# Split weights at a place in their tiles that moves by 16 bytes from piece to piece, and three raw weight buffers for four

## The chip, the cores and the metric

The kernel runs on one core of a Trainium2 chip. The metric is the device time of one execution in microseconds (us); lower is better. Beside the timed runs there is one execution under the hardware profiler, whose trace is what the rows below come from.

## The reference

The reference is the trunk of a decoder with two mixing layers, each followed by an MLP, on one sequence of 1024 positions with 1024 features, all in float32. Every layer adds its result to x.

```
for layer in range(2):
    if layer == 0: x = x + even_mixer(rms_norm(x), ...)   # sparse attention with an indexer, and forgetting attention
    else:          x = x + odd_mixer(rms_norm(x), ...)    # latent attention, and a Mamba-2 scan
    x = x + square(relu(rms_norm(x) @ w1)) @ w2           # w1 1024x4096, w2 4096x1024
```

Each mixer is a wide input projection `h @ w_in`, the attention or scan on its columns, and an output projection `o @ w_out`. Most of the arithmetic is in these matrix products with weights.

## The kernel before

Positions are worked on in two halves of 512, features in chunks of 128 on the partitions. A product with weights has to be as exact as float32 at the price of a single-pass format, so both operands are split into a rounded high part and a low part that holds the rest, and `mm3` (L271) adds three matmuls: high by high, high by low, low by high. L273, L274 and L275 are these three lines, and most of TensorE's work.

Weights come in pieces. `piece` (L282) cuts a weight block into sub-pieces of at most 1024 columns per partition (four chunks of 256 columns as a rule), 512 KB each. For each sub-piece it takes a tile `wraw` (four buffers), `whi` and `wlo` (three buffers each), loads `wraw` by a DMA on SyncE's queue (L295), and calls `split` (L254): ScalarE (ACT) writes `whi` as the rounded copy of `wraw` (L257), then VectorE (DVE), or GpSimd (POOL) in the first layer's start, writes `wlo = wraw - whi` (L258). 414 sub-pieces are handled in the whole run, one after the other through the same buffers. A `wraw` buffer is free again when its `wlo` is written, a `whi` or `wlo` buffer when the last matmul on it is done. All tiles of these tags have 4096 bytes per partition, as have those of the normed x (`xnh`, `xnl`), of the hidden values (`h`) and of the general pool.

Two functions consume pieces. `proj_f` (L302) keeps a weight slice of 128 columns stationary and streams 512 positions of x past it; it serves the MLP (`mlp`, L477, and `add_rows`, L454), the output projections and part of the input projections. `proj_t` (L315) keeps a block of 128 positions stationary and streams 256, 384 or 512 weight columns. In the trace `pm<-xnh,whi` means that the result `pm` has `xnh` moving and `whi` stationary. One piece is narrow: L691 joins 72 and 4 columns to rows of 76, so its slices for the eight chunks start 304 bytes apart in the tile.

The order of the work on each engine follows the program text, in which generators for attention and scan are advanced beside the projections by `tick`; the framework's scheduler sets semaphores and buffer waits, and may move an instruction up where an earlier one is not ready. SyncE's queue carries all weight loads, the rows of x (L77), constants (L112, L136) and the output (L1401), in order. POOL's queue carries values parked in DRAM.

Of the kernel before, what the change touches and what calls it, by code (L numbers as in the profile page):

```python
# [11 lines left out]
F32 = mybir.dt.float32  # L12
F32R = mybir.dt.float32r
# [6 lines left out]
P = 128  # L20
# [16 lines left out]
def trunk(ctx, tc, a, out):  # L37
# [7 lines left out]
    wp = ctx.enter_context(tc.tile_pool(name="wp", bufs=4))  # L45
# [208 lines left out]
    def split(hi, lo, src, scale=None, eng=None):  # L254

        if scale is None:
            act.activation(hi, src, AF.Copy)  # L257
            (eng or dve).tensor_sub(lo, src, hi.bitcast(F32))  # L258
        else:
            act.activation(hi, src, AF.Copy, scale=scale)  # L260
            dve.scalar_tensor_tensor(lo, src, scale, hi.bitcast(F32), op0=ALU.mult, op1=ALU.subtract)
# [15 lines left out]
    def rstd_of(ssq, n, over, name):  # L277

        pool.tensor_scalar(ssq, ssq, 1.0 / over, EPS, op0=ALU.mult, op1=ALU.add)
        pool.tensor_tensor(ssq, ssq, mhalf[:, :n], op=ALU.pow)  # L280

    def piece(parts, kc, n):  # L282


        subs = []
        per = min(kc, 1024 // n)
        for k0 in range(0, kc, per):
            nk = min(per, kc - k0)
            raw, hi, lo = (wp.tile([P, 1024], dt, name=nm, tag=nm, bufs=bufs)[:, :nk * n]
                           .rearrange("p (k f) -> p k f", k=nk)  # L290
                           for nm, dt, bufs in (("wraw", F32, 4), ("whi", F32R, 3), ("wlo", F32R, 3)))
            at = 0
            for ap in parts:
                w = ap.shape[-1]
                nc.sync.dma_start(raw[:, :, at:at + w], ap[k0 * P:(k0 + nk) * P].rearrange("(k p) f -> p k f", p=P))  # L295
                at += w
            split(hi, lo, raw, eng=lo_of[0])
            lo_of.append(lo_of.pop(0))
            subs.append((k0, nk, hi, lo))
        return subs  # L300
# [153 lines left out]
    def add_rows(half, w, hs, last=None, late=0):  # L454

        for n in range(4):
            subs = piece([w[:, n * 256:(n + 1) * 256]], len(hs), 256)
            if late and n == 0:
                (k0, nk, hi, lo), = subs
                cut = nk - late  # L460
                subs = [(k0, cut, hi[:, :cut], lo[:, :cut]), (k0 + cut, late, hi[:, cut:], lo[:, cut:])]

            def done(ps, c):
                x = xc(half, c)
                dve.tensor_add(x, ps, x)  # L465
                if last is not None:
                    last(c)

            proj_f((lambda k: hs[k][0], lambda k: hs[k][1]), subs,
                   [(m * P, P, lambda ps, c=n * 2 + m: done(ps, c)) for m in range(2)])  # L470
            yield
# [5 lines left out]
    def mlp(half, layer, xn, last=None):  # L477
        w1, w2 = a["mlp_w1"][layer], a["mlp_w2"][layer]
        n_blocks = DFF // 512
        hs = {}  # L480

        def up(n):
            w = piece([w1[:, n * 256:(n + 1) * 256]], 8, 256)
            pair = [new_h(), new_h()]

            def done(ps, h):
                r = tmp(name="relu")
                act.activation(r, ps, AF.Relu)  # L488
                sq = tmp(name="rsq")
                pool.tensor_mul(sq, r, r)  # L490
                split(h[0], h[1], sq)

            proj_f(xn, w, [(m * P, P, lambda ps, h=pair[m]: done(ps, h)) for m in range(2)])
            hs[n] = pair

        up(0)
        yield
        for fb in range(n_blocks):
            up(2 * fb + 1)
            yield  # L500
            if fb + 1 < n_blocks:
                up(2 * fb + 2)
                yield
            yield from add_rows(half, w2[fb * 512:(fb + 1) * 512, :], hs.pop(2 * fb) + hs.pop(2 * fb + 1),
                                *((last, 2) if fb == n_blocks - 1 else ()))
# [173 lines left out]
    def qk_pair(xn, w_ap, gain, dst):  # L679

        w = piece([w_ap], 8, 256)
        st = g([P, NB, 256], name="st")
        ss = small(NB * 2, "ss")
        proj_t(xn, w, 256, lambda b, ps: head_norms(ps, b, st[:, b], ss, 2, P))
        rstd_of(ss, NB * 2, 128.0, "qk")
        for h in range(2):
            normed_T(st, 2, h, ss, dst[h], gain)
# [903 lines left out]
```

## Time and profile before

| | us |
|---|---|
| median of 2 timed runs | 2818.52 (2817.93 to 2819.11) |
| profiled execution, whole | 2821.86 |
| its span, first to last instruction | 2820.1 |
| TensorE busy in the span | 2734.5 |
| mean granted clock of TensorE | 0.989 of full speed |

The time of an execution is the span and a little around it. Busy time of an engine is the union of its instructions; lengths of matmuls overlap, as the next one starts before the end of the one before has been modelled, so the interval from start to start tells how fast they follow each other.

### The profile page before, as it was taken

The page shows a single profiled execution, that of the slowest core. Times are in us where ns is not written, and L with a number is a line of the kernel's source. Part 1 is how long each engine was busy: PE and PEld are TensorE (multiplying, and loading weights), DVE is VectorE, ACT ScalarE, POOL GpSimd, SP SyncE. Part 2 cuts the span into 40 slices and gives each one's busy share as a digit, 9 for nine tenths or more (in the row PEclk, how much of TensorE's full clock was granted, in tenths as well). Part 3 has the DMA queues.
Part 4 walks back from the last instruction along what each step waited for, and adds up shares of the span by engine and source line. Part 5 has one row for each costly group of instructions (what it writes and reads, how often), then busy time and mean ns, then how long its engine had stood idle before and what let it go on. Part 6 is the DMA issues. An engine that isn't in the chain of part 4 may idle for free.

```text
span 2820.1 us, 39104 instructions
## 1 busy us (share of the span) xinstructions
PE 2734.5 (97%) x14509; PEld 2334.4 (83%) x14509; DVE 1737.6 (62%) x3169; ACT 1256.2 (45%) x2446; POOL 743.9 (26%) x878
## 2 busy tenths in 40 slices
PE   7889999999999999999999999999999999999999
PEld 6888877888788898888888889888887788788887
DVE  5775456877864577764667666775467754634444
ACT  4665334599834345543333334554333323332322
POOL 5335433111100113331344410233134430110110
PEclk8999999999999999999999999999999999999999
DMA  5243433334422425853334452685433463333332
GB/s 175 75 132 120 154 111 90 105 105 142 142 69 67 164 84 156 237 184 113 113 112 140 168 185 84 178 239 177 133 97 115 136 220 94 116 97 97 98 97 68
DMA packets 302964, 365.84 MB, mean 130 GB/s; under 512 B 40611, under 2 KB 258606, under 8 KB 302774
## 3 DMA queue, kind: packets, MB, share of 16 engines
q1 hardware_dynamic: 236550, 223.51, 25.7%
q0 software_dynamic: 66224, 139.84, 15.3%
q8 instruction: 114, 1.87, 0.3%
q14 instruction: 76, 0.62, 0.1%
HBM read 292.16 MB, written 68.70 MB: 128 GB/s over the span
## 4 chain that ended last, share of the span: by engine, by line
PE 75%; DVE 9%; issue 6%; ACT 5%; POOL 3%; DMA 0%; POOLq 0%; DVEq 0%; ACTq 0%
PE pm L273 22%; PE pm L274 22%; PE pm L275 21%; PE po L548 2%; PE pa L537 2%; ACT junk L822 1%; PE pa L514 1%; DVE xr L450 1%; DVE wlo L258 1%; PE py L1339 1%; ACT whi L257 1%; DVE st L659 1%; POOL xnl L258 1%; DVE x L465 1%; POOL rsq L490 1%
## 5 line engine op out<-in xcount | busy, mean ns | idle before, releaser
L257 ACT ACTIVATE whi<-wraw 128x1024 fp32r<-128x1024 f32 (+2 forms) x414 | 434.0, 1049 | 608.4 <-PE pm L274 507.3
L258 DVE TENSOR_TENSOR wlo<-wraw,whi 128x1024 fp32r<-128x1024 f32 (+1 forms) x369 | 462.4, 1253 | 208.0 <-ACT whi L257 189.6
L273 PE MATMUL pm<-xnh,whi 128*128 128x512 f32 (+1 forms) x1360 | 547.1, 403 | 6.1 <-ACT xnh L257 4.9
L274 PE MATMUL pm<-xnl,whi 128*128 128x512 f32 (+1 forms) x1360 | 534.0, 393 | 8.6 <-DVE xnl L258 4.8
L275 PE MATMUL pm<-xnh,wlo 128*128 128x512 f32 (+1 forms) x1360 | 533.5, 392 | 0.0
L273 PE MATMUL pm<-h,whi 128*128 128x512 f32 x1024 | 409.6, 401 | 5.1 <-DVE tk L892 4.4
L274 PE MATMUL pm<-h,whi 128*128 128x512 f32 x1024 | 402.0, 393 | 0.7 <-DVE h L258 0.7
L275 PE MATMUL pm<-h,wlo 128*128 128x512 f32 x1024 | 402.0, 393 | 0.0
L465 DVE TENSOR_TENSOR x<-pm,x 128x512 f32<-128x512 f32 x336 | 230.9, 688 | 273.0 <-PE pm L275 268.8
L490 POOL TENSOR_TENSOR rsq<-relu 128x512 f32<-128x512 f32 x128 | 165.9, 1296 | 823.7 <-ACT relu L488 754.4
L274 PEld LDWEIGHTS pm<-xnl,whi 128*128 128x128 f32 (+1 forms) x1360 | 256.3, 188 | 65.4 <-POOL xnl L258 8.2
L273 PEld LDWEIGHTS pm<-xnh,whi 128*128 128x128 f32 (+1 forms) x1360 | 256.3, 189 | 58.1 <-ACT xnh L257 6.4
L275 PEld LDWEIGHTS pm<-xnh,wlo 128*128 128x128 f32 (+1 forms) x1360 | 255.8, 188 | 55.5 <-issue 0.4
L273 PE MATMUL pm<-whi,xnh 128*128 128x256 f32 x1024 | 299.8, 293 | 0.0
L275 PE MATMUL pm<-whi,xnl 128*128 128x256 f32 x1024 | 290.5, 284 | 1.9 <-POOL xnl L258 1.0
L274 PE MATMUL pm<-wlo,xnh 128*128 128x256 f32 x1024 | 290.0, 283 | 0.0
L273 PEld LDWEIGHTS pm<-h,whi 128*128 128x128 f32 x1024 | 193.3, 189 | 43.9 <-DVE tk L892 5.1
L275 PEld LDWEIGHTS pm<-h,wlo 128*128 128x128 f32 x1024 | 193.2, 189 | 41.3 <-DVE wlo L258 0.2
L274 PEld LDWEIGHTS pm<-h,whi 128*128 128x128 f32 x1024 | 193.4, 189 | 38.8 <-DVE h L258 1.7
L258 DVE TENSOR_TENSOR h<-rsq,h 128x512 fp32r<-128x512 f32 x128 | 95.1, 743 | 181.7 <-ACT h L257 180.5
L273 PEld LDWEIGHTS pm<-whi,xnh 128*128 128x128 f32 x1024 | 196.8, 192 | 3.1 <-issue 1.0
L274 PEld LDWEIGHTS pm<-wlo,xnh 128*128 128x128 f32 x1024 | 196.7, 192 | 2.9 <-issue 1.2
(651 smaller groups left out, 4518.7 us busy)
## 6 DMA issues: line engine op xcount, KB each, us to landing
wraw<-in_mlp_w_dram SPq DMA_DIRECT2D x256, 512.0 KB
wraw<-in_ev_w_in_dram SPq DMA_DIRECT2D x44, 512.0 KB
wraw<-in_od_w_in_dram SPq DMA_DIRECT2D x40, 512.0 KB
wraw<-in_od_w_out_dram SPq DMA_DIRECT2D x24, 512.0 KB
parked<-x POOLq DMA_DIRECT2D x16, 512.0 KB, 4.0
wraw<-in_ev_w_out_dram SPq DMA_DIRECT2D x16, 512.0 KB
x<-parked POOLq DMA_DIRECT2D x16, 512.0 KB, 7.6
wraw<-in_od_w_in_dram SPq DMA_DIRECT2D x32, 256.0 KB
```

The source lines that it names most:

```text
L257: act.activation(hi, src, AF.Copy)
L258: (eng or dve).tensor_sub(lo, src, hi.bitcast(F32))
L273: pe.matmul(ps, w[0], x[0], start=first, stop=False, skip_group_check=True)
L274: pe.matmul(ps, w[0], x[1], start=False, stop=False, skip_group_check=True)
L275: pe.matmul(ps, w[1], x[0], start=False, stop=last, skip_group_check=True)
L450: dve.scalar_tensor_tensor(y, xc(half, c), gain[:, c:c + 1], box["rb"], op0=ALU.mult, op1=ALU.mult)
L465: dve.tensor_add(x, ps, x)
L490: pool.tensor_mul(sq, r, r)
L514: pe.transpose(ps[:, k * P:(k + 1) * P], p[:, (k0 + k) * P:(k0 + k + 1) * P], ident)
L537: pe.matmul(ps[:, :m], q, kf(k0, m), start=(i == 0), stop=(i == len(mats) - 1))
L548: pe.matmul(po, v(k), pt[:, k, :], start=(k == 0), stop=(k == nk - 1))
L659: dve.tensor_scalar(v, v, r[:, b * heads + h: b * heads + h + 1], None, op0=ALU.mult)
```

## The change

`piece` keeps a counter of sub-pieces modulo 32. The `whi` and `wlo` parts of a sub-piece start 4 elements (16 bytes) per count further in their tiles; after 32 sub-pieces (512 bytes) the counter starts again at 0. To have room for this, the `whi` and `wlo` tiles grow from 1024 to 1152 elements (4096 to 4608 bytes per partition). The raw tiles stay at 1024 elements and offset 0, and there are three of them in place of four. Together the three tags take 39,936 bytes per partition in place of 40,960. Nothing else is changed: the same instructions, on the same engines.

```diff
@@ -279,6 +279,8 @@
         pool.tensor_scalar(ssq, ssq, 1.0 / over, EPS, op0=ALU.mult, op1=ALU.add)
         pool.tensor_tensor(ssq, ssq, mhalf[:, :n], op=ALU.pow)
 
+    phase_of = [0]
+
     def piece(parts, kc, n):
 
 
@@ -286,9 +288,12 @@
         per = min(kc, 1024 // n)
         for k0 in range(0, kc, per):
             nk = min(per, kc - k0)
-            raw, hi, lo = (wp.tile([P, 1024], dt, name=nm, tag=nm, bufs=bufs)[:, :nk * n]
+            at = phase_of[0] * 4
+            phase_of[0] = (phase_of[0] + 1) % 32
+            raw, hi, lo = (wp.tile([P, room], dt, name=nm, tag=nm, bufs=bufs)[:, at:at + nk * n]
                            .rearrange("p (k f) -> p k f", k=nk)
-                           for nm, dt, bufs in (("wraw", F32, 4), ("whi", F32R, 3), ("wlo", F32R, 3)))
+                           for nm, dt, bufs, room, at in (("wraw", F32, 3, 1024, 0), ("whi", F32R, 3, 1152, at),
+                                                          ("wlo", F32R, 3, 1152, at)))
             at = 0
             for ap in parts:
                 w = ap.shape[-1]
```

## Rows read from the trace of the kernel before

**Rows 1.** The page: the length of the span, and under it the busy time of each engine, its share of the span in brackets and its count of instructions; then TensorE's granted clock in 40 equal slices of the span, in tenths of full speed (9 is 90% or more).
```profile
span 2820.1 us, 39104 instructions
...
PE 2734.5 (97%) x14509; PEld 2334.4 (83%) x14509; DVE 1737.6 (62%) x3169; ACT 1256.2 (45%) x2446; POOL 743.9 (26%) x878
...
PEclk8999999999999999999999999999999999999999
```

**Rows 2.** The page's chain of work that ended last, followed back from the last instruction: its shares by engine, then by line.
```profile
PE 75%; DVE 9%; issue 6%; ACT 5%; POOL 3%; DMA 0%; POOLq 0%; DVEq 0%; ACTq 0%
PE pm L273 22%; PE pm L274 22%; PE pm L275 21%; PE po L548 2%; PE pa L537 2%; ACT junk L822 1%; PE pa L514 1%; DVE xr L450 1%; DVE wlo L258 1%; PE py L1339 1%; ACT whi L257 1%; DVE st L659 1%; POOL xnl L258 1%; DVE x L465 1%; POOL rsq L490 1%
```

**Rows 3.** The groups of instructions by line with shapes kept apart, TensorE's matmuls on weights (`out<-moving,stationary`; `128*128` is the stationary block, `128x512` the result). After the bar: busy us, mean ns of one instruction from its start to its modelled end, then the idle time before them. Of each kind the L273 row alone; L274 and L275 have the same counts.
```profile
L273 PE MATMUL pm<-xnh,whi 128*128 128x512 f32 x1344 | 539.9, 403 | 3.9 <-ACT xnh L257 2.8 <-DVE sums L524 1.1
L273 PE MATMUL pm<-h,whi 128*128 128x512 f32 x1024 | 409.6, 401 | 5.1 <-DVE tk L892 4.4 <-ACT h L257 0.7
L273 PE MATMUL pm<-whi,xnh 128*128 128x256 f32 x1024 | 299.8, 293 | 0.0
...
L273 PE MATMUL pm<-y,whi 128*128 128x512 f32 x128 | 49.9, 390 | 0.4 <-DVE x L465 0.4
L273 PE MATMUL pm<-oa,whi 128*128 128x512 f32 x64 | 26.7, 419 | 0.3 <-ACT oa L257 0.3
L273 PE MATMUL pm<-oc,whi 128*128 128x512 f32 x64 | 25.1, 392 | 0.0
L273 PE MATMUL pm<-whi,low 128*128 128x384 f32 x48 | 16.5, 344 | 0.0
L273 PE MATMUL pm<-ho,whi 128*128 128x512 f32 x32 | 14.2, 444 | 0.0
L273 PE MATMUL pm<-whi,low 128*128 128x512 f32 x32 | 13.1, 410 | 2.0 <-ACT vt L1128 2.0
L273 PE MATMUL pm<-ob,whi 128*128 128x512 f32 x32 | 12.6, 393 | 0.3 <-DVE x L465 0.3
```

**Rows 4.** The timeline of TensorE in a long stretch of the last layer without a pause (start us, length us, engine, line, operation): the first and the last of fourteen matmuls in a row on 128-column weight slices.
```profile
2599.92 0.39 PE L273 MATMUL pm<-h,whi 128*128 128x512 f32 x1
...
2602.87 0.39 PE L274 MATMUL pm<-xnl,whi 128*128 128x512 f32 x1
```

**Rows 5.** The same view in a projection with the weights moving, 256 columns wide: the first and the last of nine matmuls in a row.
```profile
1819.80 0.28 PE L275 MATMUL pm<-whi,xnl 128*128 128x256 f32 x1
...
1820.76 0.28 PE L274 MATMUL pm<-wlo,xnh 128*128 128x256 f32 x1
```

**Rows 6.** The same view at the one piece whose slices are 76 columns wide (L691): from its second matmul to its last, 23 matmuls in a row.
```profile
379.93 0.40 PE L274 MATMUL pm<-xnl,whi 128*76 128x512 f32 x1
...
384.98 0.39 PE L275 MATMUL pm<-xnh,wlo 128*76 128x512 f32 x1
```

**Rows 7.** The same view right behind a pause on TensorE (four transposes came between): the third to the last matmul of one block, nine in a row.
```profile
1800.88 0.40 PE L273 MATMUL pm<-xnh,whi 128*128 128x512 f32 x1
...
1802.72 0.39 PE L275 MATMUL pm<-xnh,wlo 128*128 128x512 f32 x1
```

**Rows 8.** The same view in the stretch at the start in which the granted clock was 0.5: nine matmuls in a row.
```profile
25.50 0.63 PE L274 MATMUL pm<-xnl,whi 128*128 128x512 f32 x1
...
28.91 0.63 PE L273 MATMUL pm<-xnh,whi 128*76 128x512 f32 x1
```

**Rows 9.** The groups by line with shapes kept apart, the two halves of a split: ACT writes `whi`, DVE writes `wlo`.
```profile
L258 DVE TENSOR_TENSOR wlo<-wraw,whi 128x1024 fp32r<-128x1024 f32 x361 | 456.4, 1264 | 208.0 <-ACT whi L257 189.6 <-PE pa L1294 10.0 <-PE py L1339 4.4
L257 ACT ACTIVATE whi<-wraw 128x1024 fp32r<-128x1024 f32 x404 | 427.1, 1058 | 605.9 <-PE pm L274 505.3 <-issue 48.6 <-PE pm L275 39.2
```

**Rows 10.** Who waited for whom (us in total, times, longest us): first ACT, then, from the same view of SyncE's own queue, the issue of the weight loads.
```profile
ACT whi L257 <- PE pm L274: 507.3, 218, 11.4
SPq L295 <- DVE wlo L258: 1748.8, 295, 22.8
```

**Rows 11.** Three timelines of one steady stretch: SyncE's weight loads (five issues merged in one row, from the first start to the last end), ACT's and DVE's work on the pieces.
```profile
2560.76 22.13 SPq L295 DMA_DIRECT2D wraw<-in_mlp_w_dram  x5
2575.83 1.23 DVE L258 TENSOR_TENSOR wlo<-wraw,whi 128x1024 fp32r<-128x1024 f32 x1 [1.93 <-ACT whi L257]
2574.73 1.06 ACT L257 ACTIVATE whi<-wraw 128x1024 fp32r<-128x1024 f32 x1 [1.56 <-PE pm L274]
2580.17 1.06 ACT L257 ACTIVATE whi<-wraw 128x1024 fp32r<-128x1024 f32 x1
```

**Rows 12.** The DMA issues by tile (all from POOL's queue): count, KB of one and the median us from issue to landing, where the trace tells the landing.
```profile
parked<-x POOLq DMA_DIRECT2D x16, 512.0 KB, 4.0
...
oc<-oc POOLq DMA_DIRECT2D x8, 512.0 KB, 11.9
```

**Rows 13.** Busy time of each engine in two stretches (stretch, its us, then PE, PEld, DVE, ACT, POOL with their counts of instructions; the last three numbers are the granted clock, the busy share of the 16 DMA engines and GB/s).
```profile
1118.00:1150.00 32.00, 31.60 (x187) 28.12 (x186) 21.06 (x58) 16.39 (x51) 10.04 (x13) 1.00 0.87 224
2295.00:2320.00 25.00, 25.00 (x112) 20.69 (x111) 11.91 (x14) 4.25 (x4) 4.20 (x8) 1.00 1.09 377
```

**Rows 14.** The timelines of SyncE and TensorE around the second half's rows of x.
```profile
154.65 2.46 SPq L77 DMA_DIRECT2D xrow<-in_x_dram  x4
165.78 0.37 SPq L295 DMA_DIRECT2D wraw<-in_ev_w_in_dram  x1
171.08 1.04 PE L381 MATMUL pm<-ident,xrow 128*128 128x128 f32 x8
```

## The prediction

> **What bounds the kernel now.** I read the page's first part, then its chain, then the groups of matmuls, and only then single matmuls in the timeline. TensorE is busy for 2734.5 of 2820.1 us (97%) and the granted clock is at its upper level (2.4 GHz) in all slices but the first [rows 1]. The chain that ended last lies on TensorE for 75%, and 65% of the span is the three lines of `mm3`, L273 to L275 [rows 2]. So time can come only from the interval at which matmuls on weights follow each other, or be lost by letting TensorE wait. Who waits for weights? Not TensorE: ACT's split waits for TensorE to free a `whi` buffer (507.3 us), and SyncE's loads wait for the split to free a `wraw` buffer (1748.8 us) [rows 10]. Weights are always early.
>
> The interval is start to start; the lengths of 0.39 us overlap. In a settled stretch, 14 matmuls start within 2.95 us, 0.2269 us apiece [rows 4]; 512 columns at 2.4 GHz would be 0.2133, so 13.6 ns come on top. With 256 columns it is 0.96 us over 8 intervals, 0.1200 [rows 5], against 0.1067: 13.3 ns on top, the same for half the columns. At the lower clock, 1.2 GHz, 8 intervals take 3.41 us, 0.4263 [rows 8], against 0.4267: nothing on top. That fixed sum per matmul is what a shift of addresses could touch, as the next stationary block is read while the present moving operand is read.
>
> **The change part by part.**
>
> *Addresses of `whi` and `wlo`.* Before, every tile of the pools that hold x, hidden values and weights is 4096 bytes, and a weight slice starts at a multiple of 512 bytes in its tile (128 or 256 columns of 4 bytes, or a row of 256, 384 or 512). So both operands of nearly every `mm3` matmul have the same place modulo 512 bytes. After, the weight operand is off by 0, 16, ... 496 bytes, a new value for each of the 414 tiles, while x and the hidden values stay. The counts, three lines each [rows 3]: weights stationary under 512 moving columns 3 x (1344+1024+128+64+64+32+32) = 3 x 2688 = 8064; weights moving, 3 x 1024 = 3072 of 256 columns, 3 x 48 of 384 and 3 x 32 of 512. Together 11,376.
>
> Is a shifted weight slice shown anywhere before? Once: the piece of 76 columns has rows of 304 bytes, so its k-th slice starts at 304 k bytes, which modulo 512 is 0, 304, 96, 400, 192, 496, 288, 80: eight places, multiples of 16 like those of the change. Its 23 matmuls from 379.93 to 384.98 are 22 intervals in 5.05 us, 0.2295 [rows 6]. That is 2.6 ns over the settled 0.2269, and far from 0.2133. The pause on TensorE just ahead of it does not explain it away: right behind another pause, with the old addresses, the interval is 1.84 us over 8, 0.2300 [rows 7], but there such blocks come back to 0.2269 within about ten matmuls, and the 76-column piece did not in 23. What may explain it instead is the width of 76. So the upper end is 8064 x 2.6 ns = 21 us and the lower end 0, where the width is the cause. Some matmuls run at the slower interval today already (mean lengths of 403 and 401 against 390 for the undisturbed `y` row, in part from waits [rows 3]), which brings the upper end down. I take the middle, +10 us.
>
> For weights as the moving operand no row shows a shift. The nearest row is again the 76-column one: 2.6 ns either way on 3072 + 144 + 96 = 3312 matmuls is 9 us; I take 0 and keep plus and minus 9.
>
> The Trainium skill, "SBUF — State Buffer", section "Who interferes with whom", gives TensorE two independent read ports and says that PE and ACT never wait on anyone; by that rule the shift changes nothing at TensorE and the first term is 0 in place of 10. The 76-column row speaks mildly against it, without excluding it.
>
> *Writing and reading the shifted tiles on ACT, DVE and POOL.* A split is 1058 ns on ACT and 1264 ns on DVE [rows 9], for 404 and 361 of them. No row shows one at a shifted address; the ends I keep are 0 and +10% (100 to 130 ns), which is 414 x 0.13 = 54 us of DVE work. DVE is busy for 62% and ACT for 45% [rows 1], and a split starts long before its piece is needed, since it is TensorE that it waits for [rows 10]. What hides it is that lead of more than one piece; cost on the path 0, and if the cover were gone in a tenth of the pieces, 5 us.
>
> *Three raw buffers for four.* A load is issued when the split of the piece four before it is done. In the steady stretch one piece takes (22.13 - 0.37)/4 = 5.44 us from issue to issue, as ACT's splits do: 2580.17 - 2574.73 = 5.44 [rows 11]. The DVE half that starts at 2575.83 and ends at 2577.06 frees the buffer; the load that takes it is split four pieces later, at 2574.73 + 4 x 5.44 = 2596.5, some 19.4 us after its issue. With three buffers it is 14.0 us. A load of 512 KB needs 4.0 to 11.9 us in the like-sized rows of the other queue [rows 12], so it still lands before its split. Where both queues crowd, at 1118 and at 2295 us, the DMA engines are taken up to 0.87 and beyond 1.00 [rows 13]; there the lead could shrink to nothing. But what is late then is ACT's split, which itself leads TensorE by up to three pieces of `whi` (16 us), and a crowd lasts 25 to 32 us. Cost 0; with the whole lead gone for one piece in each of the two crowds, 2 x 5.44 = 11 us is the upper end.
>
> Other loads queue behind the weights on SyncE. The one with a customer on TensorE is the second half's x: issued at 154.65, with the next weight load at 165.78 and TensorE's transposes of it from 171.08 [rows 14]. If a weight load ahead of it in the queue has to wait one buffer longer, it goes at about 165.8, 11 us later; it had 16 us until its use and needs about 12 of them by the like-sized row, so TensorE could stand for up to 7 us. I take 0, as other work fills that place.
>
> *Sum.* 10 + 0 + 0 + 0 = +10 us; ends -9 and +21 + 9 + 5 + 11 + 7 = +53 us. The profiled execution took 2821.86 us (span 2820.1 and 1.8 around it), 3.3 above the median 2818.52 of the two timed runs. The terms are increments, so I put them on the median: 2828.5, forecast 2828 us.
>
> **The rivals.**
>
> *Nothing happens at TensorE* (the width of 76 was the cause). For it: intervals at the old addresses always settle at 0.2269 whichever tile is read. Time 2818 us, from 2811 to 2822.
>
> *The fixed 13.4 ns is a clash of the two reads at equal places, and the shift dissolves it.* For it: it is the same at 256 and 512 columns, and absent at the lower clock [rows 4, 5, 8]. Against it: the 76-column row had seven of eight slices shifted and kept 0.2295 [rows 6]. Dissolved in half of the places: 11,376 x 6.7 ns = 76 us, 2742 us; in all: 152 us, 2666 us. Over 2% (56 us) it needs 4.9 ns per matmul. The Trainium skill, "TensorE: Matmul & The Clock Gate", section "Back-to-back issue gap", gives columns/2.4 + 2.5 ns for a single matmul when warm, 215.8 ns here; as an estimate from that, 11 ns per matmul would be there to win, 126 us. The trace's 226.9 doesn't agree with it, and nothing shows that addresses are the reason.
>
> *The shift makes the reads clash where they don't now.* Slower: today all slices share one place and may happen to be the good one. For it: the 76-column row is slower, not faster, and the blocks behind a pause show that the interval can be pushed up [rows 6, 7]. Against: neither goes beyond 0.2300. Its price is 13.4 ns more on all 11,376, 152 us, 2971 us; it crosses 2% from 4.9 ns more per matmul, an interval of 0.2318 in place of 0.2269.
>
> *The third raw buffer is missed.* Loads land behind their splits and TensorE waits in the crowded stretches: ends summed above, up to 11 + 7 us beside the rest, 2836 to 2846 us; against it stands the lead of 14 us.
>
> **How the numbers follow.** About 2% is what a measurement of this kernel can tell from no change. Chances: the small loss 0.44 (its own range 2819 to 2850), nothing at TensorE 0.20, dissolved clash 0.18 (of which 0.14 gain over 2%), new clash 0.13 (of which 0.10 lose over 2%), missed buffer 0.05 (0.01 over 2%). So faster 0.14, slower 0.11, same 0.75. The range takes in the upper end of the sum, 2818.5 + 53 = 2872, and below it the part of the dissolved clash with up to 4.5 ns of gain, 11,376 x 4.5 = 51 us: 2768 to 2872 us leaves out about 2 in 10.
>
> **What would show it.** Right: settled intervals of 0.228 to 0.230 in the last layer's long stretches where they are 0.2269 now, no new waits of TensorE on `whi`, `wlo` or x, SyncE's loads issued one piece later, splits of 1.06 and 1.2 us as before. Wrong: an interval that depends on the tile (some pieces at 0.215, others at 0.227), or one above 0.232, or idle time of ACT ahead of `whi` that ends with a DMA.

## The result and the profile after

| | us |
|---|---|
| before, median of 2 | 2818.52 |
| predicted (range) | 2828 (2768 to 2872) |
| after, median of 2 (2851.65 to 2852.50) | 2852.07 |
| ratio after / before | 1.0119, 95% interval 1.0076 to 1.0163 |

The changed kernel is 33.5 us slower (21 to 46 us by the interval): 1.2%, within the 2% that was forecast, but 24 us above the forecast and 2 us above the likeliest case's own range. (In the later runs the kernel before took 2822.6 to 2823.6 us; each run below is compared with that of its own session.)

The page of the changed kernel: span, busy times, and the chain by engine; they answer to [rows 1, 2].

```profile
span 2850.8 us, 39105 instructions
...
PE 2762.2 (97%) x14509; PEld 2335.0 (82%) x14509; DVE 1738.2 (61%) x3169; ACT 1255.6 (44%) x2446; POOL 743.5 (26%) x878
...
PE 77%; DVE 8%; issue 5%; ACT 4%; POOL 3%; DMA 1%; POOLq 0%; DVEq 0%; SPq 0%; ACTq 0%
```

TensorE is busy for 27.7 us more with the same 14,509 matmuls; every other engine's busy time is as before. So the same matmuls follow each other more slowly. In the chain DMA has 1% where it had 0%.

Groups of the changed kernel by line with shapes kept apart, answering to [rows 3] and [rows 9] (busy us, mean ns of one, idle before).

```profile
L273 PE MATMUL pm<-xnh,whi 128*128 128x512 f32 x1344 | 544.6, 406 | 4.0 <-DVE xr L455 2.8 <-DVE sums L529 1.2
L273 PE MATMUL pm<-h,whi 128*128 128x512 f32 x1024 | 413.2, 404 | 4.5 <-DVE tk L897 4.0 <-ACT h L257 0.5
L273 PE MATMUL pm<-whi,xnh 128*128 128x256 f32 x1024 | 300.4, 293 | 0.2 <-DVE st L658 0.2
...
L258 DVE TENSOR_TENSOR wlo<-wraw,whi 128x1024 fp32r<-128x1024 f32 x361 | 456.7, 1265 | 215.3 <-ACT whi L257 195.7 <-PE pa L1299 10.2 <-PE py L1344 4.5
L257 ACT ACTIVATE whi<-wraw 128x1024 fp32r<-128x1024 f32 x404 | 427.2, 1058 | 635.5 <-PE pm L274 523.6 <-issue 47.8 <-PE pm L275 39.6
```

Lengths rise by 3 ns where the weights are stationary under 512 columns (406 for 403, 404 for 401). Lengths overlap, so intervals tell more. The timeline of TensorE in the last layer of the changed kernel: first and last of fifteen matmuls in a row on a piece that starts 112 bytes into its tile (counted modulo 256 bytes), then first and last of fourteen in a row on pieces at 176 and 192 bytes.

```profile
2625.01 0.39 PE L273 MATMUL pm<-h,whi 128*128 128x512 f32 x1
...
2628.28 0.39 PE L275 MATMUL pm<-h,wlo 128*128 128x512 f32 x1
...
2649.91 0.39 PE L275 MATMUL pm<-xnh,wlo 128*128 128x512 f32 x1
...
2652.88 0.39 PE L273 MATMUL pm<-h,whi 128*128 128x512 f32 x1
```

That is 3.27/14 = 0.2336 us, and 25 us later 2.97/13 = 0.2285, where [rows 4] had 0.2269 in the same layer of the kernel before: the interval now depends on the piece. Taking every such interval of the trace (start to start, both matmuls on weights, pauses left out) and sorting them by the place of the piece gives this table, in ns; places 256 bytes apart are joined, as they agree within 2.4 ns (0 bytes 227.3, 256 bytes 227.9; 96 and 352 bytes 233.9 and 234.2; the furthest apart are 16 and 272 bytes, 227.6 and 230.0).

```
place, bytes mod 256     0    16    32    48    64    80    96   112   128   144   160   176   192   208   224   240
stationary, 512 moving 227.6 228.8 233.0 233.1 233.2 232.0 234.0 233.1 232.9 233.2 233.3 230.2 229.4 232.5 233.1 228.7
```

The mean is 231.83 where the kernel before has 228.07. With the weights moving, 256 columns, the mean falls: 118.16 for 119.71, lowest at 192 bytes (115.8; 114.0 at 448).

Waits of ACT in the changed kernel, whole run (us, times, longest), beside [rows 10]:

```profile
ACT whi L257 <- PE pm L274: 525.6, 220, 9.9
...
ACT whi L257 <- DMA wraw<-in_od_w_in_dram: 15.1, 4, 4.7
```

The second row had no counterpart of its size before (1.2 us, once, at 1835 us): three raw buffers let the split stand for a load. So there are two suspects, places and raw buffers, and the experiments take them one at a time.

### The profile page after: what moved, and what is told of

Its sections match the earlier page's. It is cut to its first block, busy times and chain, and to the rows that moved or that the text cites. A ratio compares the mean times of both kernels' runs of the same rounds, so it can differ in the third digit from the quotient of the medians.

```text
span 2850.8 us, 39105 instructions
## 1 busy us (share of the span) xinstructions
PE 2762.2 (97%) x14509; PEld 2335.0 (82%) x14509; DVE 1738.2 (61%) x3169; ACT 1255.6 (44%) x2446; POOL 743.5 (26%) x878
## 4 chain that ended last, share of the span: by engine, by line
PE 77%; DVE 8%; issue 5%; ACT 4%; POOL 3%; DMA 1%; POOLq 0%; DVEq 0%; SPq 0%; ACTq 0%
PE pm L274 22%; PE pm L273 22%; PE pm L275 22%; PE po L553 3%; PE pa L542 3%; PE pa L519 1%; ACT junk L827 1%; PE py L1344 1%; POOL xnl L258 1%; DVE st L664 1%; DVE wlo L258 1%; DVE xr L455 1%; POOL rsq L495 1%; DMA wraw<-in_od_w_in_dram 1%; ACT whi L257 1%
## 5 line engine op out<-in xcount | busy, mean ns | idle before, releaser
L273 PE MATMUL pm<-xnh,whi 128*128 128x512 f32 (+1 forms) x1360 | 551.5, 407 | 6.2 <-DVE xr L455 2.8
L274 PE MATMUL pm<-xnl,whi 128*128 128x512 f32 (+1 forms) x1360 | 539.7, 397 | 8.3 <-DVE xnl L258 5.2
L275 PE MATMUL pm<-xnh,wlo 128*128 128x512 f32 (+1 forms) x1360 | 537.8, 396 | 0.0
L273 PE MATMUL pm<-h,whi 128*128 128x512 f32 x1024 | 413.2, 404 | 4.5 <-DVE tk L897 4.0
L274 PE MATMUL pm<-h,whi 128*128 128x512 f32 x1024 | 405.4, 396 | 0.6 <-DVE h L258 0.4
L275 PE MATMUL pm<-h,wlo 128*128 128x512 f32 x1024 | 404.8, 395 | 0.0
L274 PEld LDWEIGHTS pm<-xnl,whi 128*128 128x128 f32 (+1 forms) x1360 | 256.9, 189 | 67.8 <-DVE xnl L258 7.2
L273 PEld LDWEIGHTS pm<-xnh,whi 128*128 128x128 f32 (+1 forms) x1360 | 257.0, 189 | 62.6 <-ACT xnh L257 6.5
L275 PEld LDWEIGHTS pm<-xnh,wlo 128*128 128x128 f32 (+1 forms) x1360 | 256.4, 189 | 60.0 <-issue 0.4
L273 PE MATMUL pm<-whi,xnh 128*128 128x256 f32 x1024 | 300.4, 293 | 0.2 <-DVE st L658 0.2
L275 PE MATMUL pm<-whi,xnl 128*128 128x256 f32 x1024 | 289.9, 283 | 2.0 <-POOL xnl L258 1.0
L274 PE MATMUL pm<-wlo,xnh 128*128 128x256 f32 x1024 | 289.9, 283 | 0.0
L273 PEld LDWEIGHTS pm<-h,whi 128*128 128x128 f32 x1024 | 193.6, 189 | 46.3 <-DVE tk L897 4.7
L275 PEld LDWEIGHTS pm<-h,wlo 128*128 128x128 f32 x1024 | 193.1, 189 | 44.6
L274 PEld LDWEIGHTS pm<-h,whi 128*128 128x128 f32 x1024 | 193.6, 189 | 41.6 <-DVE h L258 1.6
L273 PEld LDWEIGHTS pm<-whi,xnh 128*128 128x128 f32 x1024 | 196.3, 192 | 3.5 <-issue 1.3
L274 PEld LDWEIGHTS pm<-wlo,xnh 128*128 128x128 f32 x1024 | 196.2, 192 | 2.9 <-issue 1.2
```

The costliest lines, as they stand in the source:

```text
L273: pe.matmul(ps, w[0], x[0], start=first, stop=False, skip_group_check=True)
L274: pe.matmul(ps, w[0], x[1], start=False, stop=False, skip_group_check=True)
L275: pe.matmul(ps, w[1], x[0], start=False, stop=last, skip_group_check=True)
```

## The experiments

Theories. P: the place of the weights against the moving operand sets the interval, and this is the whole loss. R: having three raw buffers for four costs, by loads that come late. (The recorded expectations call R theory B at first; later their letters mean something new in each text.) The order of TensorE's matmuls is that of the kernel before in all runs but the last two, where 120 of 14,509 stand at other places in it.

**Three raw buffers alone.**
```diff
-   for nm, dt, bufs in (("wraw", F32, 4), ("whi", F32R, 3), ("wlo", F32R, 3))
+   for nm, dt, bufs, room, at in (("wraw", F32, 3, 1024, 0), ("whi", F32R, 3, 1152, 0), ("wlo", F32R, 3, 1152, 0))
```


> Three raw buffers and the larger tiles, but every piece at the start of its tile. Theory P (the interval of the matmuls depends on the place of the weight slice, modulo 256 bytes, against the other operand): intervals as before, 0.227 settled, so 2818 to 2825 us; ACT waits for weight loads by some 15 us as in the changed kernel. Theory B (the third raw buffer, or the order of the work that comes with it, costs the time): about 2850 us.

Measured 2837.33 against 2823.63: ratio 1.0047 (1.0032 to 1.0062), 13.7 us. The mean interval is 228.07, to the hundredth that of before, so no place is involved: R holds for 13.7 us. Neither of the expected times came; the loss is about half of what theory B gave it. Where? The start of the k-th matmul against the same one before grows from +3.1 us at 1099 us to +9.8 at 1187, stays there to 1774, is +18.0 at 1866 and about +17 to the end. Those are the two stretches where TensorE works off the latent attention's projections beside Mamba's input. (The first 3.1 us are not the third buffer's: two kernels with four raw buffers lie nearly as far behind this one trace of the kernel before at that matmul, 2.3 us with everything moved together and 2.8 us with DVE emptying the results, both below.) So the two stretches hold 6.7 and 8.2 us, 14.9 together. Busy times in them, first the kernel before, then three raw buffers alone, then the changed kernel (stretch, its us, PE, PEld, DVE, ACT, POOL with counts, granted clock, DMA share, GB/s):

```profile
1100.00:1160.00 60.00, 59.60 (x332) 51.68 (x331) 47.96 (x97) 33.82 (x77) 22.04 (x31) 1.00 0.77 212
1820.00:1870.00 50.00, 49.59 (x284) 43.50 (x283) 37.72 (x80) 27.51 (x67) 18.77 (x20) 1.00 0.79 214
```
```profile
1100.00:1160.00 60.00, 55.99 (x295) 48.04 (x294) 43.51 (x98) 28.65 (x69) 19.31 (x28) 0.94 0.68 186
1820.00:1870.00 50.00, 44.30 (x239) 38.43 (x238) 31.86 (x72) 22.02 (x59) 16.57 (x18) 0.93 0.68 184
```
```profile
1100.00:1160.00 60.00, 57.30 (x309) 49.21 (x308) 45.43 (x101) 30.03 (x71) 21.20 (x29) 0.97 0.69 195
1820.00:1870.00 50.00, 46.05 (x251) 39.72 (x250) 34.45 (x76) 23.59 (x63) 17.71 (x19) 0.97 0.70 190
```

TensorE stands for 3.6 and 5.3 us more than before, and its granted clock falls below 1: it is 0.5 from 1146.9 to 1153.8 us and from 1853.5 to 1860.3 us. The DMA engines are less busy than before, but so is everything in these stretches, so this does not tell why the loads are late. The time from issue to landing tells more. Here is the load whose split starts at 1144.61 us, in the timeline of SyncE (two issues merged in one row, the second starting at 1129.04 us):

```profile
1126.58 5.60 SPq L296 DMA_DIRECT2D wraw<-in_od_w_in_dram  x2
```

It landed about 15.6 us after its second issue. All four waits of ACT for a load in the two stretches are for the same kind of piece, the one that joins 192 and 64 columns and is loaded by two DMAs; these landed 15.6 to 18.7 us after the second issue, while the splits would have started 11.1 to 14.6 us after it. With four raw buffers the same pieces were split 16.4 to 18.6 us after it, just enough: ACT waited once, for 1.2 us. Why this kind takes so long was not tested. The timeline of three raw buffers alone shows how a late load reaches TensorE:

```profile
1142.69 0.39 PE L275 MATMUL pm<-whi,low 128*128 128x512 f32 x1
1142.98 1.70 PE L665 MATMUL pa<-ident,qst 128*128 128x128 f32 x8
1144.61 1.06 ACT L257 ACTIVATE whi<-wraw 128x1024 fp32r<-128x1024 f32 x1 [4.46 <-DMA wraw<-in_od_w_in_dram]
1145.58 0.26 ACT L1125 ACTIVATE junk<-pm 128x128 f32<-128x128 f32 x1
...
1147.07 0.68 ACT L1129 COPY vt<-pm 128x256 f32<-128x256 f32 x2
1147.53 0.79 PE L273 MATMUL pm<-whi,low 128*128 128x512 f32 x1 [2.84 <-ACT vt L1129]
1148.12 0.63 PE L274 MATMUL pm<-wlo,low 128*128 128x512 f32 x1
1148.54 0.63 PE L275 MATMUL pm<-whi,low 128*128 128x512 f32 x1
...
1149.82 0.63 PE L275 MATMUL pm<-whi,low 128*128 128x512 f32 x1
```

ACT stands for 4.46 us for a load, then splits a piece that TensorE doesn't need yet. Behind it in ACT's order wait the squares (`junk`) and the copy (`vt`) that empty the result of a projection out of PSUM, the memory that TensorE writes its results to; the weights of that projection have long been there. TensorE has no free result buffer and waits for `vt`, 2.84 us. The same wait in the kernel before, from 1095 to 1195 us (us, times, longest):

```profile
PE pm L273 <- ACT vt L1128: 0.4, 1, 0.4
```

After that pause its matmuls start 0.42 us apart, the interval of 1.2 GHz in [rows 8], until 1153.7 us. That reading is tested further down.

**Every piece at one place, 96 bytes.** Both parts start at element 24; three raw buffers.
```diff
+                           for nm, dt, bufs, room, at in (("wraw", F32, 3, 1024, 0), ("whi", F32R, 3, 1152, 24),
+                                                          ("wlo", F32R, 3, 1152, 24)))
```


> As the changed kernel, but every piece lies 96 bytes into its tile, always the same. Theory P: the changed kernel's trace has 234.0 ns per interval at 96 and at 352 bytes against 228.1 on average before, on 8064 matmuls: 48 us, so 2866 us, worse than the changed kernel. Theory D (the step from piece to piece upsets a rhythm that would settle at any fixed place): 2818 to 2825 us, settled intervals of 0.227. Theory B: about 2850 us.

Measured 2872.47: ratio 1.0176 (1.0161 to 1.0191). Mean interval 234.14, no variation of the place. Timeline of this kernel in the last layer:

```profile
2651.83 0.40 PE L274 MATMUL pm<-xnl,whi 128*128 128x512 f32 x1
...
2655.11 0.40 PE L273 MATMUL pm<-xnh,whi 128*128 128x512 f32 x1
```

3.28/14 = 0.2343. So it is not the changing of the place from piece to piece that costs, but the place itself.

**Everything moved together.** A tile ahead of the pools grows by 24 elements, so that weights, x and hidden values all lie 96 bytes further; four raw buffers.
```diff
-    mhalf = lead.tile([P, 224], F32, name="mhalf")
+    mhalf = lead.tile([P, 248], F32, name="mhalf")
```


> The kernel before with one tile at the bottom of the memory larger by 96 bytes, so that weights, x, hidden values and all else lie 96 bytes further together; four raw buffers. Theory P, with the place of the two operands against each other deciding: 2818 us, intervals of 0.227. Theory P with the absolute place of the weight slice deciding: 0.234 and 2866 us.

Measured 2824.19 against 2823.63, ratio 1.0000 (0.9991 to 1.0010), intervals 228.1 and 119.7. What counts is the place of the weights relative to the other operand.

**The cycle alone.** Sixteen places of 16 bytes, four raw buffers; `mhalf` is cut to 16 elements to make room.
```diff
-    mhalf = lead.tile([P, 224], F32, name="mhalf")
+    mhalf = lead.tile([P, 16], F32, name="mhalf")
...
+            phase_of[0] = (phase_of[0] + 1) % 16
...
+                           for nm, dt, bufs, room, at in (("wraw", F32, 4, 1024, 0), ("whi", F32R, 3, 1088, at),
+                                                          ("wlo", F32R, 3, 1088, at)))
```


> The shifting places alone: sixteen places of 16 bytes (256 bytes, the period seen in the changed kernel's trace) in tiles of 1088 elements, and four raw buffers; the room comes from a constant tile at the bottom that is smaller by 832 bytes, which moves everything together. If places and raw buffers add up: 8064 x 3.8 ns more and 3072 x 1.5 ns less, +25 us, a ratio of 1.009, and no wait of ACT for weight loads. If the shift costs nothing without the missing buffer: 1.000. If all of the change comes from the places: 1.012.

Measured 2842.91 against 2823.43: ratio 1.0072 (1.0058 to 1.0085), 19.5 us, with intervals of 231.83 and 118.13 as in the changed kernel, though all tiles behind `mhalf` lie 832 bytes lower, and ACT waits for no weight load of note. The lag behind the kernel before grows little by little to 20 us, most in the long MLP stretches. The two parts of the change add up, 1.0047 x 1.0072 = 1.0119, the ratio of the whole; it fits better than it must, as the parts are known to about 0.0015 each and the whole to 0.0044.

**High parts at 96 bytes, low parts at 0**, three raw buffers, and later **low parts at 96 bytes, high parts at 0**, four raw buffers.
```diff
+   (("wraw", F32, 3, 1024, 0), ("whi", F32R, 3, 1152, 24), ("wlo", F32R, 3, 1152, 0))
```
```diff
+   (("wraw", F32, 4, 1024, 0), ("whi", F32R, 3, 1088, 0), ("wlo", F32R, 3, 1088, 24))
```


> As fixed96, but the low parts stay at the start of their tiles. Theory P, with the block that is loaded during a matmul deciding its interval: of three intervals in a row two are slow, those in which a high part is loaded (behind L275 and behind L273), at 0.234, and the one behind L274, in which the low part is loaded, is at 0.227; 2/3 of 48 us, 2850 us. If the block that is used in a matmul decided: slow behind L273 and L274, fast behind L275. If the place of both parts against each other mattered: all three alike.

> High parts at place 0, low parts 96 bytes further, four raw buffers (the lead pool's mhalf tile is cut to 16 elements for room). With both parts at 96 bytes the interval rose by 6.0 ns to 234.1, with the high parts alone there by 2.2 ns to 230.3. Theory A (each matmul pays for the place of its own stationary slice): one of the three lines pays, mean 230.0 or 230.3, the L275 interval alone at 234. Theory B (the excess is paid on a change of place between neighbours or on the pair, and the three lines share it): all three lines within 1 ns of each other, mean anywhere from 229 to 232. If the two halves add up, 6.0 - 2.2 = 3.8 ns, mean 231.9.

The first took 2846.65 (1.0082, 1.0065 to 1.0098), the second 2847.34 in one run. Timelines in the last layer, first the high parts moved, then the low parts:

```profile
2632.76 0.39 PE L273 MATMUL pm<-xnh,whi 128*128 128x512 f32 x1
...
2635.98 0.39 PE L275 MATMUL pm<-xnh,wlo 128*128 128x512 f32 x1
```
```profile
2632.26 0.40 PE L273 MATMUL pm<-xnh,whi 128*128 128x512 f32 x1
...
2635.52 0.40 PE L275 MATMUL pm<-xnh,wlo 128*128 128x512 f32 x1
```

3.22/14 = 0.2300 and 3.26/14 = 0.2329. Over the whole trace the means after L273, L274 and L275 are 229.9, 230.3 and 230.6 in the first, 233.1, 231.7 and 232.4 in the second. No line carries the cost alone, so the idea that each matmul pays for its own stationary slice falls. High parts alone add 2.2 ns, low parts alone 4.3, both 6.1: nearly a sum, but the low parts, stationary in only one matmul of three, weigh more. The excess is shared by neighbours; which pairing of reads sets it stays open. (Theory B's limits were missed as well, narrowly: the three lines lie 1.4 ns apart, not 1, and their mean is 232.4, not 232 at most.)

**Places 4 bytes apart**, 64 of them, four raw buffers, to see whether places within 16 bytes are alike.
```diff
+            at = phase_of[0]
+            phase_of[0] = (phase_of[0] + 1) % 64
```


> As cycle_raw4, but in 64 places of 4 bytes. If what counts is the 16-byte line in which a slice starts: the four places in one line have about the same mean interval, and the time is that of cycle_raw4 to 5 us. If a slice that starts inside a line touches one line more and pays for it: intervals longer by 1 to 2 ns at three of four places, 10 us more.

One run: 2837.13, mean interval 232.19. They are not alike: in the first 16 bytes 227.4 at 0, 232.3 at 4, 230.9 at 8, 230.3 at 12; over all places the range is 227.4 to 236.6, the latter at 164 bytes. The expectation of a 16-byte line was wrong; I have no rule for the finer pattern.

**Only the streamed pieces at 192 bytes.** Pieces that `proj_t` streams lie 48 elements further, pieces that stay stationary lie at 0; four raw buffers, and `mhalf` cut to 16 elements as above. `MOVING` is 48; the six other pieces of `proj_t` are called likewise.
```diff
-        w = piece([w_ap], 8, 256)
+        w = piece([w_ap], 8, 256, MOVING)
```


> A version that uses what the trace showed: pieces whose slices are stationary stay at the start of the tile, pieces that are streamed lie 192 bytes into theirs (in the changed kernel's trace 114.0 and 115.8 ns at 448 and 192 bytes against 119.7 at 0); four raw buffers. Theory P: 3072 x 4.8 ns less, 15 us, a ratio of 0.995. Theory D (a shift can only disturb): 1.000 or above.

Measured 2816.47 against 2823.43: ratio 0.9976 (0.9967 to 0.9985), 7 us faster than the kernel before, and the fastest of all. Its timeline in a projection with the weights moving, answering to [rows 5]:

```profile
1811.74 0.28 PE L274 MATMUL pm<-whi,xnh 128*128 128x256 f32 x1
...
1814.80 0.28 PE L276 MATMUL pm<-whi,xnl 128*128 128x256 f32 x1
```

3.06/26 = 0.1177 for 0.1200; over all, 116.30 for 119.71. That is 3.4 ns of the 4.8 hoped for, on 3072 matmuls 10.5 us, of which 7 were seen.

**Who empties PSUM.** To test the reading of the third buffer: DVE alone empties the key and value projection, with ACT's squares taken from DVE's copy, once with four and once with three raw buffers.
```diff
+            dve.tensor_copy(vt[:, b].rearrange("p (h d) -> p h d", h=2), v[:, :, 1])
-                act.activation(junk[:, :P], ps[:, h * 256:h * 256 + P], AF.Square,
+                act.activation(junk[:, :P], ks[:, b, h * P:(h + 1) * P], AF.Square,
-            act.copy(vt[:, b].rearrange("p (h d) -> p h d", h=2), v[:, :, 1])
```


> Four raw buffers and all places at 0, as before, but the result of the key and value projection of the latent attention is emptied from PSUM by DVE alone: DVE copies the values too, and ACT takes its squares from DVE's copy of the keys. It is the control of vtdve_raw3. Both theories: ACT never waits for a weight load in these stretches with four raw buffers, TensorE waited for ACT's value copy for about 1 us there, so the time stays within 5 us of the kernel before, 2818 to 2828.

> The same edit with three raw buffers, places at 0. Theory A (the third buffer costs 13 us because ACT, waiting for a weight load in order, holds back the emptying of PSUM behind it, and TensorE stands and then runs at half clock): ACT still waits 14 to 20 us for weight loads at 1100 to 1160 and 1820 to 1870 us, but TensorE no longer stands for the value copy, its clock stays at 1.00 in these stretches, and the loss against vtdve_raw4 falls from 13 us to 0 to 5 us. Theory B (TensorE is short of split weights because the loads come late, whoever empties PSUM): TensorE then waits for whi or wlo instead, and the loss stays at 10 to 14 us.

Measured 2824.69 with four (1.0007, 0.9998 to 1.0016) and 2830.74 with three (1.0026, 1.0015 to 1.0037), both against 2822.57. The third buffer now costs 6.0 us (1.0026 over 1.0007 is 1.0019, uncertain by about 0.0014, or 4 us), less than half of 13.7. That is 1 us above what theory A allowed, within the uncertainty. In the traces the two stretches lag by 4.7 us between these two kernels, where it was 14.9. With four raw buffers ACT did stand for weight loads for 4.5 us in all, which neither theory expected, and the time did not show it. Busy times with four, then with three raw buffers:

```profile
1100.00:1160.00 60.00, 59.38 (x332) 51.42 (x331) 49.38 (x110) 30.87 (x69) 21.20 (x29) 1.00 0.73 208
1820.00:1870.00 50.00, 49.38 (x283) 43.21 (x282) 39.36 (x85) 26.70 (x65) 19.75 (x24) 1.00 0.83 214
```
```profile
1100.00:1160.00 60.00, 57.98 (x322) 50.03 (x322) 46.69 (x106) 30.37 (x69) 19.83 (x29) 1.00 0.70 193
1820.00:1870.00 50.00, 47.35 (x266) 41.43 (x265) 37.83 (x83) 25.00 (x61) 16.72 (x21) 0.97 0.77 207
```

And the timeline of the latter at the place that was shown above:

```profile
1143.80 1.06 ACT L257 ACTIVATE whi<-wraw 128x1024 fp32r<-128x1024 f32 x1 [4.04 <-DMA wraw<-in_od_w_in_dram]
1143.82 0.42 DVE L1124 COPY kst<-pm 128x256 f32<-128x256 f32 x1
1144.15 0.41 DVE L1125 COPY vt<-pm 128x256 f32<-128x256 f32 x1
...
1144.71 0.47 PE L273 MATMUL pm<-whi,low 128*128 128x512 f32 x1 [0.62 <-DVE vt L1125]
...
1145.49 0.40 PE L273 MATMUL pm<-whi,low 128*128 128x512 f32 x1
```

ACT waits for the same load as long as before (4.04 us for 4.46), but TensorE waits 0.62 us in place of 2.84, its matmuls stay at full clock here (in the second stretch the granted clock is 0.97, where theory A had 1.00), and no matmul waits for `whi` or `wlo`. ACT's waits for these loads are 14.0 us in all, as in three raw buffers alone. So most of the third buffer's cost went through the emptying of PSUM behind the waiting split. What is left sits at the query projection, which I did not move: its PSUM is still emptied behind a split, by ACT's squares and DVE's copies, and TensorE's waits on `qrs` there are 1.4 us in the first stretch and 2.4 in the second.

```profile
PE pm L273 <- DVE qrs L1093: 1.4, 1, 1.4
```

## Why the prediction was right and where it was not

*What bounds the kernel*: right. The loss lies in TensorE's intervals and its waits: measured apart, 19.5 us for the intervals and 13.7 for the waits with the lower clock, 33.2 for the 33.5 of the whole. In the changed kernel's own trace the two crowded stretches hold 9.9 us, not 14.9, so the split of its loss is known only roughly.

*Addresses, weights stationary* (+10, ends 0 and 21): that the interval depends on the place, and the direction, were right; the term was mis-sized. The intervals rose by 3.76 ns, 30 us on 8064 matmuls; about a tenth of these start behind a pause, and summed over the rest the trace has 27.6 us, above the upper end. That the read of the next stationary block is what makes the difference, as the prediction had it, no run shows. The upper end of 2.6 ns came from the 76-column row, which is itself a mean over eight places; modulo 256 they are 0, 48, 96, 144, 192, 240, 32 and 80, and the same places average 231.4 in the table above, 4.5 ns over [rows 4]. So a 76-wide slice pays less than a 128-wide one: in the trace of the kernel before its slices at 96 and 144 bytes, three intervals each, have 228.0 ns, where 128-wide ones have 234.0 and 233.2. Taking the middle between it and 0 halved a bound that was too low already. By the rule of the Trainium skill, "SBUF — State Buffer", section "Who interferes with whom", that PE and ACT never wait on anyone, this term would have been 0. These runs do not agree with that 0: 228.1 ns at one relative place and 234.1 at another, with nothing else changed at TensorE. Whether the added time is a wait at a read port they do not show.

*Addresses, weights moving* (0, ends plus and minus 9): -1.55 ns on 3072, -4.8 us, inside the ends, and a gain. Both address terms together, 30.3 - 4.8 = 25.5 us by the counts, are 23.0 us when the intervals without a pause are summed in the trace of the cycle alone (27.6 - 4.6), and 19.5 us of time. In the other kernels it is alike: 7 of 9.9 us with the streamed pieces moved, 36 of 44.5 us for the fixed 96 bytes (1.0176 over 1.0047). So 15 to 30% of what the intervals gain or lose does not reach the end, presumably where TensorE waits for something else soon after; that was not tested, and each of the times is uncertain by some 3 to 6 us.

*Writing and reading the shifted tiles on ACT and DVE* (0): right; 1058 and 1265 ns for 1058 and 1264 [rows 9].

*Three raw buffers* (0, end 11): this step failed. It said that what is late then is ACT's split, "which itself leads TensorE by up to three pieces". It gave a load 4.0 to 11.9 us by the rows of the other queue and a lead of 14.0; the late loads needed 15.6 to 18.7. That lateness was allowed for, and it came: 15.1 us of waits on ACT. The split did have its lead, and no matmul came to wait for `whi` or `wlo`. But the split is not alone on ACT: in ACT's order the emptying of PSUM stood behind it (the timeline from 1144.61 us), and that has no lead at all. The step asked what waits for the split and left out what waits behind it. The cost was 13.7 us (9 to 17.5 by the interval), above the upper end, since a pause also brought some microseconds at half clock, which the sum of "the whole lead gone for one piece" did not hold.

*The rows of x* (0, end 7): right; TensorE waits 5.4 us for them before and after.

*The rivals.* "Nothing at TensorE" and "the clash dissolved" are out for the stationary weights: no place is below 227. The 215.8 ns that the prediction took from the Trainium skill, "TensorE: Matmul & The Clock Gate", section "Back-to-back issue gap", is reached by none. The longer interval that "new clash" foresaw is what happens, at 3.8 ns on average, short of its 4.9 ns for 2%; at a fixed 96 bytes, 6.1 ns, it would be 1.3% without the third buffer's share. "The third raw buffer is missed" was given 0.05 and happened as well. The outcome is the likeliest case with this rival on top: 2818.5 + 19.5 + 13.7 = 2851.7. I had treated the two as alternatives though both could come true at once.

*The range* held in part by luck. The two terms that cost something had upper ends of 21 and 11 us, which would end at 2850.5, and the time was above that; it lies inside 2872 only by the ends of 9, 5 and 7 us of terms that cost nothing or gained.

*What would show it.* The listed signs of a wrong forecast were seen: an interval that depends on the piece, above 0.232 for most places, and ACT idle ahead of `whi` that ends with a DMA. Of the signs of a right one, no new waits of TensorE on `whi` or `wlo` and splits as long as before were seen too.

Open: which pairing of reads sets the interval (no run separates the two read paths), the pattern below 16 bytes, and why the loads of the joined piece take so long.

## What to carry to other kernels

Before a prefetch buffer is given up, look at what stands behind the waiting instruction on its engine, not only at who needs its result: a split that leads by several pieces can hold back a copy out of PSUM that leads by nothing. If the relative place of stationary and moving operand is to be changed, try one fixed place for each kind of product and read the intervals, rather than cycle through all; of the multiples of 16 bytes, equal places were best here for stationary weights and 192 bytes for streamed ones. And an average over several places in a row of before is no upper end for a change that uses others.

## What the runs showed of the hardware

The interval of back-to-back matmuls with a new stationary slice each time depends on where the two operands lie relative to each other: at multiples of 16 bytes 227 to 234 ns at 512 columns, 114 to 120 ns at 256, repeating every 256 bytes within 2.4 ns, and unchanged when both move together. The best place is not the same for the two kinds: 0 bytes where weights are stationary, 192 bytes where they move. A stretch of 4.5 us in which TensorE did eight transposes and then stood for 2.84 us (1142.98 to 1147.53 us) was followed by some 6 us of matmuls at 0.42 us, the 1.2 GHz interval, with a granted clock of 0.5. ACT, waiting for a load, held back what stood behind it in its order: 4.46 us of its wait became 2.84 us of TensorE's, though TensorE did not need that load yet.
